# Value and gate projections of sixteen heads: from inside the head loop to a phase of seven half-size products

## The chip, the cores and the metric

The kernel runs on one core of one Trainium2 chip. The metric is the device time of one execution in microseconds (us); lower is better. The engines of the core work in parallel and each takes its own instructions strictly in the order in which they stand: TensorE (PE in the profile; its weight loads are PEld), VectorE (DVE), ScalarE (ACT), GpSimd (POOL) and SyncE (SP). SP issues most of the transfers between DRAM and the on-chip memory (SBUF), POOL issues the rest. [...]

## The reference, cut to what matters

A two-layer network on 1024 latent tokens (plus 256 context tokens) of width 1024. Layer 0 mixes neighbourhood attention and mLSTM heads; the change does not touch its code. Layer 1 is a bidirectional gated recurrence with 16 heads of key width 128 and value width 128. Of the reference, this matters:

```
def project(h):
    q, f_fwd, f_bwd, i, z = _split_cols(h @ w_in, C_SIZES)      # five blocks of 2048 columns
    ...
    rec = (silu(q) per head, i per head, (decay(f_fwd), decay(f_bwd)))
    return rec, z

def merge(o, z):
    o = _rms(o per head, h_norm)
    return (o * jax.nn.silu(z)) @ w_out
```

For head `h`, `q`, `f_fwd`, `f_bwd`, `i` (the value, `v` in the kernel) and `z` (the gate) are each 128 columns of a product of the normalised tokens (1280 x 1024, float32) with a weight matrix (1024 x 10240). `z` is needed for the 1024 latent tokens only, `v` for the context too. Within a head the recurrence over a chunk is computed as a masked product of queries and keys in seven levels (block sizes 1, 2, 4 ... 64), and between chunks as a scan.

## The kernel before, in words

The program is written with a tile framework. A scheduler with a timeline model of the engines orders each engine's instructions before the launch: of the instructions that it holds ready, the one that comes first in the program goes first. Once ordered, each engine runs its list in that order, so an instruction that waits holds up everything behind it on its engine.

Float32 accuracy on PE comes from splits: every operand is kept as a high and a low part in the format fp32r, and a product is three matmuls (high x high, high x low, low x high): lines 120 to 122 in `dense`. `split` (lines 69 to 72) makes the parts of a weight slab of 128 x 512 elements: a copy on ACT (line 71) and a subtraction on DVE (line 72). `wblock` and `wring` load slabs and split them; a ring of `slabs` = 4 buffers for each part holds the weights of two projections of 128 columns.

Layer 0 ends with its output projection (lines 731 to 733, `out_tile`), the normalisation of layer 1 and the transposes that fill `hh` and `hl`, the high and low parts of the normalised tokens, transposed (`mod_tr`, `h_sink`; code lines 1148 to 1156). While PE is at that, the first projections of head 0 are already mixed in (`wf`).

Then the head loop (lines 1163 to 1170) runs 16 times:

- `hg_proj(h)` forms the two decays `F` and the queries `q`: for each direction 256 + 512 + 512 columns of tokens, for the queries 512 + 512, each of 24 matmuls (8 depth steps x 3). Weights stand still in the array, tokens move through.
- `hg_intra` runs the seven levels for two halves of 512 tokens. `hg_level` is a chain across engines: ACT gathers keys (`gksel`, line 895), PE forms scores in four matmuls (line 900), DVE copies the scores of this level under a mask into `A` (line 910) and scales `Q` and `K` in place by four products with the running decay (line 918), which the next level needs.
- `hg_vz(h)` makes `v` and `z`: a block of 256 columns (128 of `v`, 128 of `z`) as four slabs `wzh`, `wzl`; 24 matmuls with 256 moving columns for the context's `v`; then for each of the eight token tiles 24 matmuls of 256 columns (tokens standing still, weights moving), a copy of `v`, a sigmoid and a product for `z` (lines 816 to 821).
- `hg_ctx` forms the state after the context, `hg_scan` runs the scan over eight chunks, the normalisation, the product with `z`, and writes the head's result to DRAM.

Between heads, buffers allow a projection of the next head to start once the first level has read `F`. After the loop the second output projection (lines 731 to 733 again) ends the kernel; its first half of depth (`out_ahead`) is ready before the last head is through and lies mixed with it.

Of the kernel before, what the change touches and what calls it, by code (L numbers as in the profile page):

```python
# [9 lines left out]
F32 = mybir.dt.float32  # L10
F32R = mybir.dt.float32r
U8 = mybir.dt.uint8
AF = mybir.ActivationFunctionType
# [5 lines left out]
P = 128  # L19
# [24 lines left out]
class Prog:  # L44
# [724 lines left out]
            self.nc.sync.dma_start(out=self.gbc[:, v, :], in_=src.partition_broadcast(P))  # L769


    def hg_proj(self, h, pool, w=None):
# [4 lines left out]
        F = [self.t(p, [P, 2, 512], F32, "gF", 1) for p in (pool, self.fp)]  # L777
        Fc = self.t(self.fp, [P, 2, CTX], F32, "gFc", 1)
        todo = [(d, t0, n) for d in range(2) for t0, n in ((LAT, CTX), (512, 512), (0, 512))]
        if w:  # L780

            todo.sort(key=lambda x: x[1] == 0)
        w = w or [None, None]
        for d, t0, n in todo:
            w[d] = w[d] or self.wring([col(1 + d)], P)
            ps = self.ps("mm", [P, n])
            self.proj_tr(ps, w[d], 0, t0, n)
            dst = Fc[:, d, :] if t0 == LAT else F[t0 // 512][:, d, :]
            nc.scalar.activation(dst, ps, AF.Sigmoid)
            nc.vector.tensor_scalar(out=dst, in0=dst, scalar1=olb, scalar2=lb, op0=ALU.mult, op1=ALU.add)  # L790
# [9 lines left out]
        return dict(F=F, Fc=Fc, q=q)  # L800

    def hg_vz(self, h, st, pool):
        nc, a = self.nc, self.a
        col = lambda i: a["wc"][:, i * 2048 + h * P : i * 2048 + (h + 1) * P]
        w = self.wblock(pool, "wz", [col(3), col(4)], KD, 256)
        v = self.t(pool, [P, NT, P], F32, "gv", 2)
        z = self.t(pool, [P, NT - 2, P], F32, "gz", 1)
        ps = self.ps("mm", [P, CTX])
        self.proj_tr(ps, w, 0, LAT, CTX)
        vT = self.t(pool, [P, CTX], F32, "gEc", 1)  # L810
        nc.scalar.copy(vT, ps)
        pt = self.ps("tr", [P, 2, P])
        for j in range(2):
            nc.tensor.transpose(pt[:, j, :], vT[:, j * P : (j + 1) * P], self.ident)
        nc.scalar.copy(v[:, 8:10, :], pt)
        for tt in range(8):
# [4 lines left out]
            nc.vector.tensor_tensor(out=z[:, tt, :], in0=z[:, tt, :], in1=ps[:, P:256], op=ALU.mult)  # L821
        st["v"], st["z"] = v, z


# [157 lines left out]
    def build(self):  # L982
        tc, nc, a = self.tc, self.nc, self.a
        dma = nc.sync.dma_start
        with ExitStack() as es:
# [7 lines left out]
            self.Gd = self.scratch(dr, "Gd", [2, 4, T])  # L993
            self.mpd = self.scratch(dr, "mpd", [2, 4, NT])
            self.x1 = self.scratch(dr, "x1", [T, D])
            self.md_all = self.scratch(dr, "md", [20, T, 256])
            self.md = {}

# [109 lines left out]
            lk = self.fp = l1.enter_context(tc.tile_pool(name="hgk", bufs=1))  # L1108
            with tc.tile_pool(name="op0", bufs=2) as op, ExitStack() as wl:
                self.gate_bc(0, op, 2, 1)  # L1110
                later = []
# [32 lines left out]
                for ld in rest:  # L1144
                    ld()
                self.slabs = 4
                wf = [self.wring([a["wc"][:, 2048 : 2048 + P]], P), None]
# [9 lines left out]
                wf[1] = self.wring([a["wc"][:, 4096 : 4096 + P]], P)  # L1157

            with l1:
                pool = l1.enter_context(tc.tile_pool(name="hg", bufs=2))  # L1160
                self.rawp = pool
                l1.enter_context(self.pp.phase(s=3, acc=1))
                st = self.hg_proj(0, pool, wf)
# [164 lines left out]
```

## Time and profile before

| what | value |
|---|---|
| three runs | 3575.16, 3577.86, 3580.52 us |
| median of the runs | 3577.86 us |
| profiled execution, from its first to its last instruction (span) | 3582.2 us |
| granted TensorE clock, mean over the span | 0.992 |
| head loop, middle heads | 92.2 us each |

The profiled execution has no separate time of its own beside its span; the span lies 4.3 us above the median of the runs. In the profile, `mm<-wzh,hh` means: an instruction writes a buffer named `mm` from buffers named `wzh` and `hh`; `128x256` is partitions x elements, `x64` the number of instructions, and after the bar stand busy time in us and the mean of one in ns. Matmuls are pipelined: the mean of one is longer than the distance between two starts, so rates are read from start times in the timeline.

### The profile page before, as it was taken

Reading aid. Unit: us, or ns where it says so; the run is one execution under the profiler, and the core shown is the slowest. Engines: PE = TensorE matmul, PEld = TensorE weight load, DVE = VectorE, ACT = ScalarE, POOL = GpSimd, SP = SyncE. Lnnn points to the kernel's source line nnn. Section 1 sums busy time; section 2 is a strip of 40 time slices with the busy share of each in tenths; the row PEclk is TensorE's granted clock in tenths of the full one; section 3 lists DMA queues with packets and bytes.
Section 4 is the critical chain, followed back from the end, with each engine's and each line's share of the span. In section 5 each row is a group of like instructions: output and inputs, shape, how many; then the busy total and the mean of one; then the engine's idle time right before and its main releaser. Section 6 shows DMA issues by size and latency. Waiting matters only on the chain.

```text
span 3582.2 us, 65593 instructions
## 1 busy us (share of the span) xinstructions
PE 3517.0 (98%) x24954; PEld 3223.1 (90%) x24954; DVE 2216.3 (62%) x5976; ACT 1419.4 (40%) x3493; POOL 456.2 (13%) x752
## 2 busy tenths in 40 slices
PE   8999999999999999998899999999999999999998
PEld 5879999999999999997788999999999999999877
DVE  5646676666744765655556666666666666666753
ACT  5545555445533333433354333333333333333431
POOL 2222222222211212201010000000000000000000
PEclk9999999999999999999999999999999999999999
DMA  5532222232234434324742111111111111111263
GB/s 211 173 99 77 83 71 81 72 90 76 80 96 145 127 94 140 116 73 149 221 145 77 36 36 34 36 36 36 36 33 36 30 36 36 33 33 36 77 192 117
DMA packets 323051, 305.25 MB, mean 85 GB/s; under 512 B 29016, under 2 KB 280088, under 8 KB 322608
## 3 DMA queue, kind: packets, MB, share of 16 engines
q1 hardware_dynamic: 290704, 217.44, 20.7%
q0 software_dynamic: 32032, 83.61, 6.9%
q8 instruction: 197, 3.23, 0.4%
q14 instruction: 118, 0.97, 0.1%
HBM read 241.49 MB, written 59.30 MB: 84 GB/s over the span
## 4 chain that ended last, share of the span: by engine, by line
PE 85%; issue 6%; DMA 4%; DVE 2%; POOL 1%; ACT 1%; SPq 0%; POOLq 0%; DVEq 0%; ACTq 0%
PE mm L122 18%; PE mm L120 18%; PE mm L121 18%; PE s L900 6%; PE acc L677 2%; PE tr L657 2%; PE mm L731 2%; PE mm L732 2%; PE mm L733 2%; PE acc L461 2%; PE s L470 2%; DMA mld<-md 1%; PE acc L451 1%; PE s L929 1%; PE acc L953 1%
## 5 line engine op out<-in xcount | busy, mean ns | idle before, releaser
L122 PE MATMUL mm<-wh,hl 128*128 128x256 f32 x2560 | 749.6, 293 | 0.3 <-DVE hl L253 0.3
L120 PE MATMUL mm<-wh,hh 128*128 128x256 f32 x2560 | 747.0, 292 | 0.0
L121 PE MATMUL mm<-wl,hh 128*128 128x256 f32 x2560 | 745.9, 291 | 0.0
L122 PEld LDWEIGHTS mm<-wh,hl 128*128 128x128 f32 x2560 | 489.1, 191 | 11.1 <-issue 4.1
L120 PEld LDWEIGHTS mm<-wh,hh 128*128 128x128 f32 x2560 | 489.3, 191 | 7.7 <-issue 1.5
L121 PEld LDWEIGHTS mm<-wl,hh 128*128 128x128 f32 x2560 | 489.2, 191 | 7.1 <-issue 0.5
L120 PE MATMUL mm<-hh,wh 128*128 128x512 f32 (+1 forms) x1216 | 448.3, 369 | 0.0
L121 PE MATMUL mm<-hl,wh 128*128 128x512 f32 (+1 forms) x1216 | 448.3, 369 | 0.0
L122 PE MATMUL mm<-hh,wl 128*128 128x512 f32 (+1 forms) x1216 | 448.1, 368 | 0.0
L122 PE MATMUL mm<-wzh,hl 128*128 128x256 f32 x1024 | 295.3, 288 | 0.0
L120 PE MATMUL mm<-wzh,hh 128*128 128x256 f32 x1024 | 294.2, 287 | 0.0
L121 PE MATMUL mm<-wzl,hh 128*128 128x256 f32 x1024 | 293.9, 287 | 0.0
L895 ACT COPY gksel<-gK 128x512 f32<-128x512 f32 x224 | 149.3, 667 | 315.5 <-PE s L900 159.7
L122 PEld LDWEIGHTS mm<-hh,wl 128*128 128x128 f32 x1216 | 229.7, 189 | 31.4
L120 PEld LDWEIGHTS mm<-hh,wh 128*128 128x128 f32 x1216 | 229.7, 189 | 31.1
L121 PEld LDWEIGHTS mm<-hl,wh 128*128 128x128 f32 x1216 | 229.7, 189 | 30.7
L900 PE MATMUL s<-gQ,gksel 128*128 128x128 f32 x1792 | 254.9, 284 | 0.0
L900 PEld LDWEIGHTS s<-gQ,gksel 128*128 128x128 f32 x1792 | 231.4, 191 | 1.3
L71 ACT CAST wh<-wraw 128x512 fp32r<-128x512 f32 x242 | 148.6, 620 | 202.3 <-PE mm L121 122.5
L731 PE MATMUL mm<-woh,yh 128*128 128x512 f32 x524 | 209.4, 400 | 11.9 <-issue 9.7
L72 DVE TENSOR_TENSOR wl<-wraw,wh 128x512 fp32r<-128x512 f32 x242 | 165.3, 689 | 87.3 <-ACT wh L71 84.9
L733 PE MATMUL mm<-woh,yl 128*128 128x512 f32 x524 | 209.4, 400 | 0.0
(316 smaller groups left out, 7463.0 us busy)
## 6 DMA issues: line engine op xcount, KB each, us to landing
wraw<-yd SPq DMA_DIRECT2D x144, 256.0 KB
wraw<-in_wab_dram SPq DMA_DIRECT2D x112, 256.0 KB
md<-ev POOLq DMA_DIRECT2D x100, 256.0 KB, 2.7
wraw<-in_wc_dram SPq DMA_DIRECT2D x96, 256.0 KB
adar<-in_wada_dram POOLq DMA_DIRECT2D x32, 512.0 KB, 4.6
wraw<-in_wc_dram SPq DMA_DIRECT2D x128, 128.0 KB
adar<-in_wada_dram SPq DMA_DIRECT2D x16, 512.0 KB
wraw<-in_wab_dram SPq DMA_DIRECT2D x64, 128.0 KB
```

The source lines that it names most:

```text
L71: nc.scalar.copy(hi, x)
L72: nc.vector.tensor_tensor(out=lo, in0=x, in1=hi.bitcast(F32), op=ALU.subtract)
L120: mm(ps, lhsT=lh(k), rhs=rh(k), start=(k == 0), stop=False)
L121: mm(ps, lhsT=lh(k), rhs=rl(k), start=False, stop=False)
L122: mm(ps, lhsT=ll(k), rhs=rh(k), start=False, stop=(k == nk - 1))
L461: nc.tensor.matmul(num, lhsT=qc[:, j, :], rhs=C[d][:, j, :], start=False, stop=(j == 1))
L470: nc.tensor.matmul(u, lhsT=st["k"][c][:, j * P : (j + 1) * P], rhs=vw, start=True, stop=True)
L657: nc.tensor.transpose(pt[:nk, i, :], pr[:, o : o + nk], self.ident)
L731: mm(ps, lhsT=yh[:, k, :], rhs=w.h(kk), start=(kk == 0), stop=False)
L733: mm(ps, lhsT=yl[:, k, :], rhs=w.h(kk), start=False, stop=(kk == 8 * len(qs) - 1))
L895: nc.scalar.copy(ksel.rearrange("p (b s i) -> p b s i", s=2, i=h), pick(K))
L900: nc.tensor.matmul(pa[:, c, :].rearrange("p (b s i) -> p b s i", s=2, i=h), lhsT=ksel[:, c * P : (c + 1) * P], rhs=qp[:, c * nbc : (c + 1) ...
```

## The change

- A phase ahead of the head loop computes `v` and `z` of all heads for the 1024 latent tokens and writes them to DRAM (`vzd`). It goes through the 2048 + 2048 columns in eight blocks of 256 + 256.
- The first block (`q_plain`) is computed as before, by 2 x 8 x 24 matmuls; its first weights (`early`) are loaded while layer 0's output projection runs, in place of head 0's first decay weights (`wf`).
- Each of the other seven blocks (`q_seven`) is seen as a product of 2 x 2 halves: tokens (0 to 511, 512 to 1023), depth (0 to 511, 512 to 1023) and columns (`v`, `z`). It is formed by seven products of halves in place of eight, of 4 x 12 matmuls each.
- Four of the seven need sums and differences of halves of the tokens; `q_sums` makes them once, on DVE and ACT, split into high and low parts. Sums of halves of the weights are made for each block (`q_form`), and the products are combined on DVE (`q_out` and the lines around it). Results leave through POOL's DMA queue, 128 transfers of 128 x 256.
- In the loop `hg_vz` loads `v` and `z` of the head by two transfers on SP and still computes the context's `v`, with two slabs of its own from the ring (`wring`) in place of the four of `wz`.
- `hg_proj` loses the early start of head 0, and `F`, `Fc` move into the loop's pool with the same number of buffers. `z` gets two buffers in place of one. During the new phase PSUM has four banks `sa` beside two `mm` and two `tr`.

```
-        w = self.wblock(pool, "wz", [col(3), col(4)], KD, 256)
         v = self.t(pool, [P, NT, P], F32, "gv", 2)
-        z = self.t(pool, [P, NT - 2, P], F32, "gz", 1)
+        z = self.t(pool, [P, NT - 2, P], F32, "gz", 2)
+        for t, i in ((v, 0), (z, 1)):
+            nc.sync.dma_start(
+                out=t[:, 0:8, :], in_=self.vzd[i, :, h * P : (h + 1) * P].rearrange("(c p) f -> p c f", p=P)
+            )
+        w = self.wring([a["wc"][:, 3 * 2048 + h * P : 3 * 2048 + (h + 1) * P]], P)
...
-        for tt in range(8):
-            ps = self.ps("mm", [P, 256])
-            self.proj_nat(ps, w, tt, 0, 256)
-            nc.scalar.copy(v[:, tt, :], ps[:, 0:P])
-            nc.scalar.activation(z[:, tt, :], ps[:, P:256], AF.Sigmoid)
-            nc.vector.tensor_tensor(out=z[:, tt, :], in0=z[:, tt, :], in1=ps[:, P:256], op=ALU.mult)
...
+    def q_form(self, raw, n, add=None):
+        w = _W([], [], 2, 256)
+        for i in range(2):
+            if add:
+                self.nc.vector.tensor_tensor(out=raw[n][i], in0=raw[n][i], in1=raw[add][i], op=ALU.add)
+            w.lo.append(self.t(self.wp, [P, 512], F32R, "wl", self.slabs))
+            w.hi.append(self.t(self.wp, [P, 512], F32R, "wh", self.slabs))
+            self.split(w.hi[i], w.lo[i], raw[n][i])
+        return w
...
+        def product(a, w):
+            for i in range(4):
+                ps = self.q_ps()
+                self.q_mul(ps, a(i), w, True, True)
+                yield i, ps
+
+        u, v, m5 = {}, {}, {}
+        for i, ps in product(lambda i: self.q_h(i, 0), self.q_form(raw, "11")):
+            u[i] = self.t(pool, [P, 256], F32, "qu", 4)
+            nc.scalar.copy(u[i], ps)
+        for i, ps in product(lambda i: self.q_h(i, 1), self.q_form(raw, "21")):
+            self.q_out(pool, i, j, 0, u[i], ps, ALU.add)
+        for i, ps in product(s("1"), self.q_form(raw, "11", "12")):
+            m5[i] = ps
+        for i, ps in product(s("2"), self.q_form(raw, "11", "22")):
+            tt(out=u[i], in0=u[i], in1=ps, op=ALU.add)
+            v[i] = self.t(pool, [P, 256], F32, "qv", 4)
+            tt(out=v[i], in0=m5[i], in1=u[i], op=ALU.subtract)
+        for i, ps in product(s("3"), self.q_form(raw, "12", "22")):
+            self.q_out(pool, i + 4, j, 1, v[i], ps, ALU.subtract)
+            tt(out=u[i], in0=u[i], in1=ps, op=ALU.add)
+        for i, ps in product(lambda i: self.q_h(i + 4, 1), self.q_form(raw, "11", "21")):
+            self.q_out(pool, i + 4, j, 0, u[i], ps, ALU.add)
+        for i, ps in product(s("4"), self.q_form(raw, "22")):
+            self.q_out(pool, i, j, 1, v[i], ps, ALU.add)
...
+                with tc.tile_pool(name="qv", bufs=1) as pool, self.pp.phase(sa=4):
+                    self.q_plain(0, early, pool)
+                    S = self.q_sums(pool)
+                    for j in range(1, 8):
+                        self.q_seven(j, S, pool)
```

More of the change, by code (lines that the diff above doesn't have):

```diff
@@ L776, in hg_proj @@
         lb, olb = self.lb[:, 0, h : h + 1], self.lb[:, 1, h : h + 1]
-        F = [self.t(p, [P, 2, 512], F32, "gF", 1) for p in (pool, self.fp)]
-        Fc = self.t(self.fp, [P, 2, CTX], F32, "gFc", 1)
+        F = [self.t(pool, [P, 2, 512], F32, "gF", 2) for _ in range(2)]
+        Fc = self.t(pool, [P, 2, CTX], F32, "gFc", 1)
         todo = [(d, t0, n) for d in range(2) for t0, n in ((LAT, CTX), (512, 512), (0, 512))]
-        if w:
-            todo.sort(key=lambda x: x[1] == 0)
-        w = w or [None, None]
+        w = [None, None]
         for d, t0, n in todo:
@@ new lines, in q_raw @@
+    def q_raw(self, pool, j):
+        nc, raw = self.nc, {}
+        for n in ("11", "21", "12", "22"):
+            c0 = (3 if n[1] == "1" else 4) * 2048 + j * 256
+            raw[n] = []
+            for i in range(2):
+                r = self.t(pool, [P, 512], F32, f"b{n}", 4 if n == "11" else 2)
+                k0 = (int(n[0]) - 1) * 512 + i * 256
+                nc.sync.dma_start(
+                    out=r.rearrange("p (k f) -> p k f", f=256),
+                    in_=self.a["wc"][k0 : k0 + 256, c0 : c0 + 256].rearrange("(k p) f -> p k f", p=P),
+                )
+                raw[n].append(r)
+        return raw
@@ new lines, in q_form, with q_mul @@
+    def q_form(self, raw, n, add=None):
+        w = _W([], [], 2, 256)
+        for i in range(2):
+            if add:
[4 more added lines that the diff above has]
+        return w
+    def q_mul(self, ps, a, w, first, last):
+        mm = self.nc.tensor.matmul
+        ah, al = a
+        for k in range(4):
+            mm(ps, lhsT=ah[:, k, :], rhs=w.h(k), start=first and k == 0, stop=False)
+            mm(ps, lhsT=ah[:, k, :], rhs=w.l(k), start=False, stop=False)
+            mm(ps, lhsT=al[:, k, :], rhs=w.h(k), start=False, stop=last and k == 3)
@@ new lines, in q_ps, with q_plain @@
+    def q_ps(self):
+        self.nq += 1
+        return self.ps("sa" if self.nq % 8 < 4 else "mm" if self.nq % 2 else "tr", [P, 256])
+    def q_plain(self, j, early, pool):
+        raw = self.q_raw(pool, j)
+        for z in range(2):
+            w = early if early and not z else [self.q_form(raw, f"{k}{z + 1}") for k in (1, 2)]
+            for c in (4, 0):
+                for i in range(4):
+                    ps = self.ps("sa", [P, 256])
+                    for k in range(2):
+                        self.q_mul(ps, self.q_h(c + i, k), w[k], k == 0, k == 1)
+                    self.q_out(pool, c + i, j, z, ps)
@@ new lines, in q_seven @@
+    def q_seven(self, j, S, pool):
+        nc = self.nc
+        raw = self.q_raw(pool, j)
+        s = lambda n: lambda i: [t[:, :, i * P : (i + 1) * P] for t in S[n]]
+        tt = nc.vector.tensor_tensor
+        def product(a, w):
+            for i in range(4):
+                ps = self.q_ps()
[20 more added lines that the diff above has]
+            self.q_out(pool, i, j, 1, v[i], ps, ALU.add)
@@ L1146, in build @@
                 self.slabs = 4
-                wf = [self.wring([a["wc"][:, 2048 : 2048 + P]], P), None]
+                early = []
+                for k in range(2):
+                    rows = a["wc"][k * 512 : (k + 1) * 512, 3 * 2048 : 3 * 2048 + 256]
+                    early.append(self.wblock(self.wp, "w", [rows], 4, 256, op, ring=self.slabs))
                 for tt in [8, 9, 4, 5, 6, 7, 0, 1, 2, 3]:
```

57 lines of the change are left out of this document (52 added, 5 removed).

## The prediction

> **What bounds the kernel now.** I read the page first (busy shares, chain), then stages of the span, then one middle head by shapes, then that head's timelines of TensorE and VectorE.
>
> ```profile
> span 3582.2 us, 65593 instructions
> PE 3517.0 (98%) x24954; PEld 3223.1 (90%) x24954; DVE 2216.3 (62%) x5976; ACT 1419.4 (40%) x3493; POOL 456.2 (13%) x752
> ...
> PE 85%; issue 6%; DMA 4%; DVE 2%; POOL 1%; ACT 1%; SPq 0%; POOLq 0%; DVEq 0%; ACTq 0%
> ...
> L122 PE MATMUL mm<-wzh,hl 128*128 128x256 f32 x1024 | 295.3, 288 | 0.0
> L120 PE MATMUL mm<-wzh,hh 128*128 128x256 f32 x1024 | 294.2, 287 | 0.0
> L121 PE MATMUL mm<-wzl,hh 128*128 128x256 f32 x1024 | 293.9, 287 | 0.0
> L71 ACT CAST wh<-wraw 128x512 fp32r<-128x512 f32 x242 | 148.6, 620 | 202.3 <-PE mm L121 122.5
> L72 DVE TENSOR_TENSOR wl<-wraw,wh 128x512 fp32r<-128x512 f32 x242 | 165.3, 689 | 87.3 <-ACT wh L71 84.9
> ...
> md<-ev POOLq DMA_DIRECT2D x100, 256.0 KB, 2.7
> ```
>
> PE holds 85% of the chain. The three rows of 1024 are the work that the change moves: 3072 matmuls, 192 a head. The stages (columns: span; busy of PE, PEld, DVE, ACT, POOL; clock; DMA share; GB/s):
>
> ```profile
> 1778.00:1791.00 13.00, 3.26 (x9) 2.40 (x8) 6.05 (x9) 3.66 (x7) 0.54 (x1) 0.60 0.74 242
> 1852.00:1948.00 96.00, 96.00 (x472) 80.88 (x471) 60.22 (x150) 50.55 (x124) 8.46 (x18) 1.00 0.39 117
> 2500.07:2592.27 92.20, 92.20 (x652) 86.07 (x652) 60.40 (x150) 29.99 (x74) 4.28 (x6) 1.00 0.12 35
> 3376.00:3389.00 13.00, 12.47 (x58) 10.25 (x59) 10.00 (x21) 7.32 (x12) 0.00 (x0) 0.87 1.03 311
> ```
>
> A middle head is 92.2 us with PE full; DVE is busy 60.4. An average hides that DVE's work is not spread evenly over the head. Shapes of that head, and PE's and DVE's timelines in its seven levels:
>
> ```profile
> L120 PE MATMUL mm<-wzh,hh 128*128 128x256 f32 x64 | 18.4, 287 | 0.0
> L900 PE MATMUL s<-gQ,gksel 128*128 128x128 f32 x114 | 16.4, 285 | 0.0
> L895 ACT COPY gksel<-gK 128x512 f32<-128x512 f32 x14 | 9.3, 667 | 20.9 <-PE s L900 10.3 <-issue 5.0 <-DVE gK L861 3.2
> L918 DVE TENSOR_TENSOR gK<-gK,gT 128x256 f32<-128x256 f32 x24 | 9.0, 417 | 0.0
> L910 DVE COPY_PREDICATED gA<-glm,s 128x512 f32<-128x512 uint8 x12 | 8.9, 742 | 4.3 <-PE s L900 4.1
> L973 DVE SCALAR_TENSOR_TENSOR gyn<-acc,gss,gz 128x128 f32<-128x128 f32 x8 | 2.4, 345 | 0.9 <-POOL gss L147 0.6 <-PE tr L976 0.3
> L959 DVE SCALAR_TENSOR_TENSOR gS<-gS,gT,s 128x128 f32<-128x128 f32 x7 | 2.4, 347 | 7.6 <-PE acc L954 5.2 <-PE s L957 2.4
> L147 POOL TENSOR_TENSOR gss<-gss,mhalf 128x4 f32<-128x4 f32 x2 | 2.4, 1194 | 0.2
> L979 POOL DMA_DIRECT2D yd<-gyt x2 | 1.2, 600 | 19.4 <-ACT gyt L978 10.6 <-DVE gz L821 8.8
> L835 DVE TENSOR_SCALAR gq<-gFc 128x512 f32<-128x512 f32 x1 | 0.4, 414 | 0.0
> L790 DVE TENSOR_SCALAR gF<-gF,lb 128x512 f32<-128x512 f32 x4 | 2.2, 542 | 0.0
> ```
>
> ```profile
> 2508.25 0.61 PE L929 MATMUL s<-gq,gksel 128*128 128x128 f32 x4
> ...
> 2515.12 0.28 PE L121 MATMUL mm<-wzl,hh 128*128 128x256 f32 x1
> ...
> 2517.96 0.28 PE L121 MATMUL mm<-wzl,hh 128*128 128x256 f32 x1
> 2518.08 1.06 PE L900 MATMUL s<-gQ,gksel 128*128 128x128 f32 x8
> 2518.89 0.36 PE L122 MATMUL mm<-wzh,hl 128*128 128x256 f32 x1
> ...
> 2539.23 1.06 PE L900 MATMUL s<-gQ,gksel 128*128 128x128 f32 x8
> ```
>
> ```profile
> 2519.17 0.75 DVE L910 COPY_PREDICATED gA<-glm,s 128x512 f32<-128x512 uint8 x1 [0.94 <-PE s L900]
> 2519.82 0.73 DVE L918 TENSOR_TENSOR gQ<-gQ,gT 128x256 f32<-128x256 f32 x2
> 2520.48 0.74 DVE L918 TENSOR_TENSOR gK<-gK,gT 128x256 f32<-128x256 f32 x2
> 2521.15 0.27 DVE L821 TENSOR_TENSOR gz<-gz,mm 128x128 f32<-128x128 f32 x1
> 2521.35 0.73 DVE L910 COPY_PREDICATED gA<-glm,s 128x512 f32<-128x512 uint8 x1
> ```
>
> From 2515.12 to 2517.96 stand 25 matmuls of 256 columns: 0.118 us from start to start (their mean of 287 ns is pipelined). A score group costs PE 0.81 us (2518.08 to 2518.89). A masked copy and two pairs of products per half level cost DVE 0.65 + 0.66 + 0.67 = 1.98 us. So in the levels DVE is nearly always busy, and PE's own share, 0.81 in about 2 us, is less than half. The rest of PE's time there is filled by exactly the matmuls that the change takes out: between 2508.25 (behind the first level's groups) and 2539.23 (the last group) lie 149 matmuls of `hg_vz`.
>
> **The change, part by part.**
>
> *PE's count.* Out: 3072 x 0.118 = 362.5 us. In: the plain block 2 x 8 x 24 = 384, seven blocks of 7 x 4 x 12 = 336, together 2736, x 0.118 = 322.8. The shape is the same (128 x 128 standing, 256 moving). Net **-39.7 us**.
>
> *The head loop without its filler.* In the order in which the changed kernel's instructions stand on PE, the score groups of levels 1 to 6 of heads 1 to 14 follow each other with nothing between them but the 24 matmuls of the context's `v`, two pairs of transposes, and near the end the transposes of `K`; the next head's projections stand in front of this stretch or behind it. Working per head:
> - PE's own work without the 192: 92.2 - 22.7 = 69.5 us.
> - Of it inside the stretch: 30.98 us (2508.25 to 2539.23) - 149 x 0.118 = 13.4, plus 24 x 0.118 = 2.8 for the context: 16.2. Outside: 53.3, still back to back as far as the order shows.
> - DVE's list inside it, between the scores of level 0 and the last group: 24 pairs (L918) x 0.66 = 15.9, 13 masked copies x 0.64 = 8.3, four `gyn` (0.345 each), one level-0 product, one `gF` (0.542), one `gq` (0.414): about 2.8. Sum **27.0 us**, on one engine in order. PE cannot leave it sooner, since the last group needs the last but one pair.
> - Handing over at both ends 0.6 us (a group's 1.06 us against its 0.81, and a wait on ACT).
>
> Period 53.3 + 27.0 + 0.6 = 80.9. DVE's waits for PE inside the stretch were 4.1 us a head (L910's row); without the filler in PE's queue they should shrink, but a group still needs a 0.667 us gather on ACT first. Bounds 0 to 4.1; I take 1.3, nearer to none because what DVE waited for was mostly the filler: **82.2 us, PE idle 12.7** (11.4 to 15.5). Times 14 heads: **+178** (160 to 217). What DVE sheds per head, two slab splits and eight gate products, lies mostly outside the stretch and is worth nothing while PE is the bound there.
>
> *Head 0 and head 15.* Head 0's levels have projections of head 1 between them, and head 15's the second output projection's first half (192 matmuls), which before covered head 15's scan. That scan then stands bare: seven state steps of PE and DVE (L959, 0.347 us, plus a matmul and handing over, about 0.8 each), two normalisations with POOL's 1.2 us, the write (2.7 us to land) and reading back. About 25 us, of which PE's own matmuls fill some 10. **+15** (5 to 25).
>
> *The new phase.* Per seven-product block PE 336 x 0.118 = 39.6 us. DVE: 14 low parts and 8 sums of 128x512 x 0.689 + 36 combinations of 128x256 x 0.42 = 30.3. ACT: 14 x 0.62 and twelve copies or sigmoids of 256 columns, each under the 0.667 of L895's 512: at most 16.7. POOL: 16 issues x 0.6 = 9.6, with nothing else on its queue. SP: eight loads of 256 KB. The ring holds two products' weights, so a product's split (2 x (0.62 + 0.69) = 2.6 us) runs under the product before it (5.7 us). All of it is under PE; I cost it at nothing, and if that cover failed it would be up to 2.6 us per product (below). Three places are not covered:
> - the raw weights of the plain block's second half: they wait until the projection's buffers are free, 2 MB at the 240 GB/s of the stage around 1780 take 8 us, against 11 us of PE work at hand, partly waiting itself: +6 (0 to 12);
> - `q_sums`: 56 operations of DVE of 128x512, with the splits and combinations around them about 45 us, while PE has about 49 us that doesn't need them: +5 (0 to 15);
> - the seam into the loop: head 0's first weights go into memory that the phase's results occupy, so they wait for the last result's way (two DVE operations 0.84, sigmoid at most 0.67, issue 0.6, landing 2.7), then load 2.7 and split 1.3: +10 (3 to 15).
>
> Together **+21** (3 to 42). Head 0's early projections leave the stretch 1852 to 1948, where PE is full; the plain block's first matmuls take their place, both are PE work: 0. The two loads of `v`, `z` per head (1 MB) run two heads ahead on a DMA system used to 12%: 0; a late one would hold the scan.
>
> *Sum.* 3582.2 - 39.7 + 178 + 15 + 21 = 3756.5 against this execution's span; the median of the runs lies 4.3 lower: **3752 us**, 4.9% slower. With the lower bounds 3706, with the upper ones 3837.
>
> **The clock.** PE idle for a moment has a price here:
>
> ```profile
> 3376.53 1.16 PE L847 MATMUL s<-gv,gknc 128*128 128x128 f32 x8 [1.88 <-ACT gknc L842]
> ```
>
> After these 1.88 us the stage 3376 to 3389 ran at 0.87, that is 3.4 of 13 us at half. In the bare levels PE's gaps are shorter, about 1 us, but come every 2 us. [...] No stage of this trace has such a rhythm. I leave it out of the sum and make it a rival.
>
> **Rivals.**
> 1. *The clock drops in the bare levels.* Then PE's 16.2 us there grow up to 32 and pass DVE's 27: +5 us, and 3.4 us at half behind them: +1.7. Up to 6.7 x 14 = 94: 3846 us. For it: the 1.88 us gap. [...] Chance 0.13.
> 2. *The new phase starves PE.* DVE's list (30 of 39.6 us) mixes splits with combinations that wait for PE; if half of each split lies open: 49 products x 1.3 = 64, 3816 us. For it: ACT and DVE rows 71 and 72 wait for each other even now. Chance 0.10.
> 3. *Faster: PE stays full in the levels after all*, because DVE's gathered waits vanish and the next head's decays run under the levels. Period 69.5, phase and tail at their lower bounds: 3582.2 - 39.7 + 8 - 4.3 = 3546 us. It decides only if the idle per head falls under (39.7 - 21 - 15) / 14 = 0.3 us, so a period under 70. Against it: DVE's 27.0 us for 16.2 of PE, by count. Chance 0.03.
>
> **Numbers.** The forecast has 0.73; 0.01 is left for no change. What a measurement of this kernel can tell from none is about 0.2%, 7 us. The forecast's own range is 3706 to 3837; 3700 to 3840 takes in the second rival and part of the first. Faster 0.03, same 0.01, slower 0.96.
>
> **What would show it.** Right: middle heads of 81 to 84 us, in each a stretch of about 27 us with PE half idle behind DVE and score groups some 2 us apart; the new phase full on PE with products of 5.7 us; matmuls 336 fewer. Wrong: a period near 70 (rival 3), a clock under 0.95 in the loop (rival 1), PE idle between products with ACT or DVE as releaser (rival 2), or idle PE outside the levels, where I assume none.

## The result, and the profile after

The changed kernel takes **3824.19 us** (median of four executions, 3822.89 to 3830.06) where the kernel before takes 3579.19 (four executions, 3575.16 to 3580.75): **6.9% slower**, ratio 1.0688 with a 95% interval of 1.0672 to 1.0703. The forecast was 3752, with a range of 3700 to 3840. The side came out as foretold, and so did the mechanism in the head loop. But 72 us are missing from the sum, and most of them lie where the prediction had written a zero.

From the page of the changed kernel: span, busy time and instructions of each engine, the chain of waits that ended last, by engine ("issue" is time for which the profile shows no wait), and four groups (busy us and mean ns, then idle time before them and what ended it).

```profile
span 3820.8 us, 65738 instructions
PE 3586.6 (94%) x24618; PEld 3229.4 (85%) x24618; DVE 2385.5 (62%) x6294; ACT 1456.6 (38%) x3427; POOL 517.8 (14%) x880
...
PE 26%; issue 11%; DVE 11%; DMA 5%; POOL 2%; ACT 1%; SPq 0%; POOLq 0%; DVEq 0%; ACTq 0%
...
L120 PE MATMUL mm<-hh,wh 128*128 128x512 f32 (+1 forms) x1344 | 487.8, 363 | 34.4 <-ACT gFc L786 26.5
...
L1027 PE MATMUL s<-gQ,gksel 128*128 128x128 f32 x1792 | 293.3, 316 | 79.6 <-DVE gQ L1045 52.7
...
L731 PE MATMUL mm<-woh,yh 128*128 128x512 f32 x524 | 214.5, 410 | 52.2 <-ACT yh L71 35.7
...
L71 ACT CAST yh<-wraw 128x512 fp32r<-128x512 f32 x144 | 86.7, 619 | 214.3 <-DMA wraw<-yd 117.7
```

PE has the 336 matmuls fewer that were counted (24954 to 24618), and is busy for 94% of the span instead of 98%. The 26% of the chain must not be set beside the 85% of before: on this page the chain is followed back only to 1680 us, 56% of the span. From 1680 us to the end, PE holds 87% of the chain before and 46% after. So PE no longer bounds that part alone. Two of the waits are large; the same groups in the kernel before:

```profile
L900 PE MATMUL s<-gQ,gksel 128*128 128x128 f32 x1792 | 254.9, 284 | 0.0
...
L731 PE MATMUL mm<-woh,yh 128*128 128x512 f32 x524 | 209.4, 400 | 11.9 <-issue 9.7
```

Score groups (L1027; L900 before) now stand 79.6 us idle, mostly behind DVE: the levels of the head loop. And the matmuls of layer 0's output projection (L731) stand 52.2 us idle, 35.7 of them behind the splits of its `y` tiles, which in turn wait for loads: work that the change does not touch.

The stages of both kernels, cut at the same instructions: the first matmul of the last pass of layer 0's output projection, the last transposes of that stage (L229), the context transposes of head 0 and of head 14 (columns: span; busy PE, PEld, DVE, ACT, POOL; clock; DMA share; GB/s). Before:

```profile
0.00:1788.00 1788.00, 1738.25 (x13226) 1598.96 (x13227) 1088.44 (x3253) 810.54 (x2043) 365.81 (x612) 0.99 0.38 113
1788.00:1918.40 130.40, 130.39 (x615) 108.75 (x616) 76.16 (x182) 68.34 (x173) 13.71 (x28) 0.98 0.44 131
1918.40:1997.40 79.00, 79.00 (x544) 73.58 (x543) 56.81 (x139) 29.54 (x67) 0.00 (x0) 1.00 0.17 48
1997.40:3286.30 1288.90, 1288.90 (x9092) 1203.27 (x9091) 844.25 (x2100) 419.19 (x1021) 60.42 (x84) 1.00 0.12 35
3286.30:3582.20 295.90, 280.50 (x1482) 238.55 (x1480) 150.66 (x304) 91.83 (x190) 16.27 (x28) 0.98 0.40 121
```

After:

```profile
0.00:1789.50 1789.50, 1734.37 (x13226) 1594.65 (x13226) 1087.61 (x3253) 809.24 (x2043) 365.40 (x612) 0.99 0.37 114
1789.50:1978.30 188.80, 152.62 (x655) 107.18 (x656) 78.96 (x180) 69.40 (x170) 12.23 (x28) 0.98 0.29 88
1978.30:2398.10 419.80, 402.97 (x3124) 391.46 (x3123) 290.04 (x612) 139.39 (x277) 68.98 (x128) 0.98 0.29 97
2398.10:3557.00 1158.90, 1051.12 (x6414) 932.51 (x6413) 784.65 (x1960) 353.54 (x770) 54.27 (x84) 0.96 0.15 45
3557.00:3820.80 263.80, 245.55 (x1205) 203.60 (x1203) 144.27 (x290) 85.01 (x168) 16.91 (x28) 0.98 0.42 133
```

The differences of these rows against the terms of the prediction. A head's place against its context moved a little with the change, so the two outer stages are taken together; the forecast for them is 322.8 (the phase) + 21 + 15 - 2 x 22.65 (the products that left heads 0 and 15).

| stage | forecast | measured |
|---|---|---|
| up to the last pass of layer 0's projection | 0 | +1.5 |
| that pass | 0 | **+58.4** |
| new phase, lead-in of head 0, and all behind head 14 (+340.8 and -32.1) | +313.5 | +308.7 |
| 14 periods of the head loop | -139.1 | -130.0 |
| sum (span) | +174.4 | +238.6 |

So three questions went to the chip: what the 58.4 us are, whether the rest has the causes that the prediction gave, and whether the heads can have their filler back.

### The profile page after: what moved, and what is told of

The parts are those of the page before. It is cut to its first block, busy times and chain, and to the rows that moved or that the text cites. A ratio compares the mean times of both kernels' runs of the same rounds, so it can differ in the third digit from the quotient of the medians.

```text
span 3820.8 us, 65738 instructions
## 1 busy us (share of the span) xinstructions
PE 3586.6 (94%) x24618; PEld 3229.4 (85%) x24618; DVE 2385.5 (62%) x6294; ACT 1456.6 (38%) x3427; POOL 517.8 (14%) x880
## 4 chain that ended last, share of the span: by engine, by line
PE 26%; issue 11%; DVE 11%; DMA 5%; POOL 2%; ACT 1%; SPq 0%; POOLq 0%; DVEq 0%; ACTq 0%
PE mm L120 6%; PE mm L121 6%; PE mm L122 6%; DMA wraw<-yd 3%; DVE gQ L1045 3%; DVE gK L1045 3%; DVE gA L1037 2%; PE s L1027 2%; POOL vzd L883 2%; PE mm L731 1%; PE mm L733 1%; PE mm L732 1%; PE acc L1080 1%; PE acc L1081 1%; PE s L1067 1%
## 5 line engine op out<-in xcount | busy, mean ns | idle before, releaser
L120 PE MATMUL mm<-hh,wh 128*128 128x512 f32 (+1 forms) x1344 | 487.8, 363 | 34.4 <-ACT gFc L786 26.5
L122 PE MATMUL mm<-hh,wl 128*128 128x512 f32 (+1 forms) x1344 | 487.5, 363 | 0.0
L121 PE MATMUL mm<-hl,wh 128*128 128x512 f32 (+1 forms) x1344 | 487.0, 362 | 0.0
L1027 PE MATMUL s<-gQ,gksel 128*128 128x128 f32 x1792 | 293.3, 316 | 79.6 <-DVE gQ L1045 52.7
L1027 PEld LDWEIGHTS s<-gQ,gksel 128*128 128x128 f32 x1792 | 260.9, 215 | 109.0 <-ACT gksel L1022 69.3
L120 PEld LDWEIGHTS mm<-hh,wh 128*128 128x128 f32 x1344 | 257.1, 191 | 71.4 <-ACT gFc L786 29.4
L121 PEld LDWEIGHTS mm<-hl,wh 128*128 128x128 f32 x1344 | 257.3, 191 | 34.4
L731 PE MATMUL mm<-woh,yh 128*128 128x512 f32 x524 | 214.5, 410 | 52.2 <-ACT yh L71 35.7
L732 PE MATMUL mm<-wol,yh 128*128 128x512 f32 x524 | 209.0, 399 | 0.0
L731 PEld LDWEIGHTS mm<-woh,yh 128*128 128x128 f32 x524 | 99.9, 191 | 88.0 <-ACT yh L71 53.4
L71 ACT CAST yh<-wraw 128x512 fp32r<-128x512 f32 x144 | 86.7, 619 | 214.3 <-DMA wraw<-yd 117.7
```

The source lines that it names most:

```text
L71: nc.scalar.copy(hi, x)
L120: mm(ps, lhsT=lh(k), rhs=rh(k), start=(k == 0), stop=False)
L121: mm(ps, lhsT=lh(k), rhs=rl(k), start=False, stop=False)
L122: mm(ps, lhsT=ll(k), rhs=rh(k), start=False, stop=(k == nk - 1))
L731: mm(ps, lhsT=yh[:, k, :], rhs=w.h(kk), start=(kk == 0), stop=False)
L732: mm(ps, lhsT=yh[:, k, :], rhs=w.l(kk), start=False, stop=False)
```

## Experiments

**Where the 58.4 us come from.** In the changed kernel the pass's chain of waits no longer runs through PE (start, length in us, what):

```profile
1853.10 0.63 ACT yh L71
...
1854.47 2.82 DMA wraw<-yd
...
1857.31 0.63 ACT yh L71
...
1857.96 0.70 DVE yl L72
1858.68 2.81 DMA wraw<-yd
...
1861.57 0.63 ACT yh L71
```

Load, copy, subtraction, next load: one after the other, 4.2 us a round, as if there were one buffer for the raw `y` tiles. The pool has three (`wraw`). Its readers and writers in this pass, same kernel (xcount: least/median/most ns, first and last start):

```profile
L71 ACT CAST yh<-wraw x40: 617/618/621, 1788.8 to 1966.8; 128x512 fp32r<-128x512 f32 x40
...
L718 SPq DMA_DIRECT2D wraw<-yd x39: 359/360/1449, 1790.2 to 1964.0; - x39
L71 ACT CAST wh<-wraw x2: 621/622/622, 1970.1 to 1970.8; 128x512 fp32r<-128x512 f32 x2
```

The two splits of weights at 1970.1 and 1970.8 stand behind the last `y` tile. My theory was this. The ring for split weights has four slabs a part, and this pass still uses two of them for its own last slabs; `early` loads two blocks of two slabs. The first block finds slabs, the second only when the pass is over, and until then its two raw slabs lie in two of the three raw buffers. In the kernel before, `wf` took only the two slabs that were free.

*Raw buffers of their own for the early weights:*

```
-                    early.append(self.wblock(self.wp, "w", [rows], 4, 256, op, ring=self.slabs))
+                    early.append(self.wblock(self.wp, "w", [rows], 4, 256, op, 2, "eraw", ring=self.slabs))
```

> The changed kernel, with raw buffers of its own (two) for the first two weight blocks of the new phase, which are loaded during the layer-0 output projection. Theory A (these two blocks sit in two of the three raw buffers until that projection's slabs are free, so the y tiles are loaded and split one after the other through the third): the projection's last stage goes from 188.8 back to about 131 to 135 us, and the time from 3824 to about 3765 to 3770. Rival B (the stage is longer because other work stands in it: more loads and splits of weights on ScalarE and VectorE, or the projections of the plain block queued there): the stage stays above 175 us and the time at 3810 to 3825.

Measured: 3749.44 us (3746.22 to 3753.11), 75 less than the changed kernel; against the kernel before 1.0474 (1.0458 to 1.0489).

*Only the first early block ahead of the tiles, the second behind them:*

```
-                for k in range(2):
+                for k in range(1):
...
                     self.mod_tr(1, [xn], tt, op, self.h_sink(tt * P, P))
+                rows = a["wc"][512:1024, 3 * 2048 : 3 * 2048 + 256]
+                early.append(self.wblock(self.wp, "w", [rows], 4, 256, op, ring=self.slabs))
```

> The changed kernel, with only the first of the two early weight blocks loaded ahead of the tiles of the layer-0 output projection, the second behind them. Theory A (raw buffers held): the first block takes the slabs that are free and gives its raw buffers back at once, so the stage is again 131 to 135 us long; what is loaded later costs at most 3 us at the start of the phase: about 3765 to 3772. Rival B (other work in the stage): half of the 58 us comes back at most, 3795 to 3824.

Measured: 3772.21 us (3769.26 to 3774.48), 52 less; 1.0537 (1.0519 to 1.0554). It is 23 above the first cure: 8 in front of the first tile, 8 in head periods of 83.1 in place of 82.5, the rest behind head 14.

*The kernel before, with one raw buffer for `y`:*

```
-            yr = self.t(rp or yp, [P, 512], F32, "wraw", 3).rearrange("p (j t) -> p j t", j=4)
+            yr = self.t(rp or yp, [P, 512], F32, *(("yraw", 1) if getattr(self, "oneraw", 0) else ("wraw", 3))).rearrange("p (j t) -> p j t", j=4)
...
+                self.oneraw = 1
                 for tt in [8, 9, 4, 5, 6, 7, 0, 1, 2, 3]:
```

> The kernel before, in which the y tiles of the layer-0 output projection go through one raw buffer of their own instead of sharing three. Nothing else is changed. Theory A: one raw buffer alone makes the stage as long as in the changed kernel, about 185 to 190 us instead of 130.4, and the time 3634 to 3640 instead of 3579. Rival B: the loads stay hidden behind the matmuls of each tile, the stage stays at 130 to 140 us and the time below 3590.

Measured: 3621.48 us (3612.92 to 3624.57), 1.0112 (1.0097 to 1.0127): slower by 42, not by 55 to 60.

The transposes of the pass's ten tiles tell the pace (first and last start), in this order: before, the changed kernel, own raw buffers, one early block, the kernel before with one buffer. One fence for each:

```profile
L229 PE MATMUL tr<-ident,nx x80: 270/272/276, 1811.3 to 1918.4; 128*128 128x128 f32 x80
```

```profile
L229 PE MATMUL tr<-ident,nx x80: 270/272/273, 1815.2 to 1978.3; 128*128 128x128 f32 x80
```

```profile
L229 PE MATMUL tr<-ident,nx x80: 270/272/276, 1799.1 to 1906.1; 128*128 128x128 f32 x80
```

```profile
L229 PE MATMUL tr<-ident,nx x80: 270/272/276, 1806.7 to 1914.0; 128*128 128x128 f32 x80
```

```profile
L229 PE MATMUL tr<-ident,nx x80: 270/272/276, 1800.6 to 1964.8; 128*128 128x128 f32 x80
```

Ten tiles take 107.1, 163.1, 107.0, 107.3 and 164.2 us. Both cures give the pace back whole, and one raw buffer in the kernel before, without anything of the change, makes the whole loss: **the cause is the number of raw buffers that the `y` tiles find free**, and rival B of the three expectations is out. The single-buffer kernel shows the same wait, a 2.8 us load between two splits of each `y` tile:

```profile
L71 ACT CAST yh<-yraw 128x512 fp32r<-128x512 f32 x36 | 22.2, 618 | 69.5 <-DMA yraw<-yd 64.0 <-PE mm L733 3.4 <-PE mm L732 2.0
```

My sizes missed by what stands ahead of the pass. With raw buffers of its own (third and fifth row) the first tile is 11 to 12 us earlier than before; so the first cure gave 75 us and not 55 to 60, and the single buffer cost 42 and not 55. The prediction had shown that hole without asking for its cause: the row 1778 to 1791, PE busy 3.26 of 13 us.

*The kernel before, with two raw buffers for `y` and two for the weights in place of three shared:*

```
-            rw = rawp if isinstance(rawp, list) else (rawp or self.rawp, rawb, rawt)
+            rw = rawp if isinstance(rawp, list) else (rawp or self.rawp, getattr(self, "rb", rawb), rawt)
...
-            yr = self.t(rp or yp, [P, 512], F32, "wraw", 3).rearrange("p (j t) -> p j t", j=4)
+            yr = self.t(rp or yp, [P, 512], F32, *(("yraw", 2) if getattr(self, "oneraw", 0) else ("wraw", 3))).rearrange("p (j t) -> p j t", j=4)
...
-                raws[:] = [op, 3, "wraw"]
+                raws[:] = [op, 2, "wraw"]
+                self.rb = 2
...
+                self.oneraw = 1
```

> The kernel before, in which the y tiles of the layer-0 output projection have two raw buffers of their own and the weights two others, instead of three shared. Nothing else changes. In the runs with y buffers of their own the first tile's transposes stood at 1799 to 1801 us instead of 1811, also where y had only one. Theory A (the start of that stage waits for raw buffers that weights hold): with two y buffers the tiles keep 12 us each and the start is 11 to 12 us earlier, 3566 to 3570 instead of 3579.6. Rival B (the 12 us at the start are taken back in front of the head loop, as 6.5 of the 46.4 us were in the run with one buffer, or two buffers are too few for a tile in 12 us): 3575 to 3590.

Measured: **3567.40 us** (3564.53 to 3568.86), 0.9958 (0.9944 to 0.9972): the one version here that is faster than both kernels. It differs from the kernel before in two things at once: the pools are separate, and there are four raw buffers in place of three. Which of the two gives the 14 us was not tried apart. The same 13 us in it, PE full where it had been idle:

```profile
1778.00:1791.00 13.00, 13.00 (x59) 10.72 (x58) 5.18 (x8) 3.98 (x7) 0.54 (x1) 1.00 0.79 234
```

**What the seven products are worth.** All eight blocks computed plainly:

```
-                    S = self.q_sums(pool)
                     for j in range(1, 8):
-                        self.q_seven(j, S, pool)
+                        self.q_plain(j, None, pool)
```

> The changed kernel, in which all eight column blocks of the new phase are computed plainly (no sums of halves, no seven products). 336 matmuls more of 0.118 us are +39.6 us; without the sums of x ahead of the phase about -5. Theory A (the phase is bound by TensorE): 3824 + 35 = 3855 to 3864. Rival B (the seven products pay their saving back to VectorE and ScalarE, which make the sums and put the products together): 3815 to 3835, no more than 10 us above the changed kernel.

Measured: 3872.38 us (3871.86 to 3872.60), 48 above the changed kernel (1.0816, 1.0800 to 1.0833). The phase with the lead-in of head 0:

```profile
1981.30:2441.20 459.90, 444.32 (x3460) 433.71 (x3458) 126.36 (x262) 115.03 (x247) 69.25 (x128) 0.98 0.26 88
```

459.9 against 419.8: +40.1 for 336 matmuls, 0.119 us each. PE bounds the phase, and the saving arrives whole, although with the seven products DVE has 290.0 us of work in place of 126.4. So rival B is out; but the 5 us that I had set for `q_sums` are not there either. The other 8 us, by which it is above theory A's figure too, are mostly the 14 head periods, which came out at 83.1 instead of 82.8 (+5).

**What bounds a head.** In the changed kernel a middle head takes 82 to 84 us. PE's waits in one of them (head from 2565.6):

```profile
L120 PE MATMUL mm<-hh,wh 128*128 128x512 f32 x48 | 19.7, 411 | 1.8 <-ACT gFc L786 1.8
...
L1027 PE MATMUL s<-gQ,gksel 128*128 128x128 f32 x112 | 17.9, 309 | 6.0 <-DVE gQ L1045 3.6 <-ACT gksel L1022 1.6 <-DVE gQ L991 0.6
```

The kernel with raw buffers of its own for the early weights has nearly the same heads (82.5 us in the mean of 14, against 82.8) and is the base of what follows. The core of its levels, and the rest of the head behind them:

```profile
2712.90:2729.10 16.20, 13.84 (x85) 12.53 (x86) 16.20 (x42) 5.69 (x10) 0.00 (x0) 0.79 0.05 18
2729.10:2737.35 8.25, 5.89 (x29) 4.60 (x28) 4.45 (x12) 1.19 (x4) 0.00 (x0) 1.00 0.01 2
```

DVE is busy 16.20 of 16.20 us, as the prediction had it. What its sum had not (it stood there as rival 1): the clock of 0.79, that is 6.8 us at half. To see whether DVE's list sets the time, its products of one level were left out, from this base and from the kernel before (the output is then another one):

```
             (Qv, 0, 0, Tv[:, 1, :, 1]), (Qv, 1, 1, Tv[:, 0, :, 0]),
         ):
+            if lev == 3:
+                continue
```

> The changed kernel with raw buffers of its own for the early weights, in which the fourth of the seven levels leaves out its multiplications of K and Q by the segment products (the output is then another one). That takes eight VectorE instructions of about 0.41 us from each head, 3.3 us, and nothing from TensorE or ScalarE. Theory A (in the levels VectorE's list sets the period now that the value and gate products are gone): the middle heads go from 82.5 to about 79 us and the time from 3749 to about 3698 to 3704. Rival B (what binds a level is the round from its matmuls over ScalarE's copy to the next matmuls, or TensorE's own work): periods 81.5 to 82.5 us, 3735 to 3750.

> The kernel before with the same eight multiplications left out of each head (the output is then another one). Theory A (TensorE is full in its levels, and VectorE's list lies beside it): periods stay at 92.0 to 92.3 us and the time within 5 us of 3580. If VectorE's list counted here too, 3.3 us a head would show: 3530.

Measured: in the base 3732.41 us (3729.22 to 3735.08), 17 less and not 45 to 51, between the two theories and nearer to B; periods of 81.6 to 82.3. In the kernel before 3578.58 (3576.11 to 3582.80), ratio 1.0004 (0.9994 to 1.0013): nothing, as both had it. The same two windows of a head without the products:

```profile
2707.70:2723.90 16.20, 13.19 (x92) 12.12 (x92) 15.47 (x38) 6.31 (x11) 0.00 (x0) 0.89 0.05 18
2723.90:2732.00 8.10, 6.34 (x21) 4.99 (x22) 2.63 (x8) 0.68 (x3) 0.00 (x0) 0.79 0.01 2
```

From the diagonal's scores behind the first level (L1056) to the last score group it is 24.3 to 25.1 us, against 26.4: in the mean of 14 heads the levels are 1.8 us shorter, for 2.5 us less of DVE in the head shown (53.47 against 55.98). In the kernel before, where PE is full, the same cut changes nothing. So DVE does set the levels. But the clock moved: 3.4 us at half are now in the window *behind* the levels (0.79 of 8.1), in every head. What that costs can be read from the base itself. Four of its 14 heads have such a spell behind the levels and take 83.4 to 83.8 us, the other ten 81.8 to 82.3: 1.3 to 1.7 us. So the head keeps 0.6 us of its 1.8 (81.9 in the mean against 82.5). My expectation priced DVE and left the clock out.

Then idle matmuls in the levels, to keep PE busy and to see whether the clock then stays up, with and without the cut:

```
         pa = self.ps("s", [P, 4, P])
+        if lev:
+            for c in range(4):
+                nc.tensor.matmul(pa[:, c, :], lhsT=self.ident, rhs=self.ident, start=True, stop=True)
```

> The run with the eight multiplications left out, and ahead of the four matmuls of each half's level (levels 2 to 7) four idle matmuls of the identity with itself into the same PSUM tile, which the true ones then write over: 48 matmuls a head, 0.11 us each, 5.3 us of TensorE work that stands where TensorE waits for VectorE. Theory C (VectorE does set the levels, which were 2.0 us shorter without the multiplications, but a half-clock window of 3.4 us behind the levels took 1.7 us of it back; with TensorE kept busy the clock stays at full speed): no half-clock windows in most heads, periods 79.5 to 80.5 us instead of 81.9, the time 3700 to 3715 instead of 3732. Rival B (a level is bound by its own round, or by TensorE's work): the added matmuls lengthen the heads, periods 82 to 87 us, 3735 to 3800.

> The changed kernel with raw buffers of its own for the early weights and the same idle matmuls, nothing left out. Theory C: the half-clock windows of 6.8 us in the levels go, but they lay beside VectorE's list and cost nothing; only the four heads of 83.4 to 83.8 us, which had a second window behind the levels, fall to 82: periods 81.5 to 82.1 us, the time 3738 to 3749 instead of 3749. Rival B: the added 5.3 us of TensorE work show, periods 84 to 88 us, 3775 to 3830. If the clock had cost its whole window (6.8 us at half speed, 3.4 us a head), periods would fall to 78.6 and the time to 3700.

Measured: 3786.88 us (3783.38 to 3791.54) and 3799.81 (3794.98 to 3801.30), both slower; the middle heads take 83.5 to 85.1 us, and 85.3. A head of the second, in the levels and behind them:

```profile
2713.50:2723.50 10.00, 10.00 (x89) 10.00 (x88) 9.76 (x26) 3.70 (x6) 0.85 (x1) 1.00 0.20 59
2723.50:2739.70 16.20, 16.20 (x147) 16.20 (x146) 15.31 (x40) 6.09 (x10) 0.61 (x1) 1.00 0.11 38
...
2744.70:2748.20 3.50, 3.02 (x7) 2.44 (x8) 1.35 (x4) 0.66 (x2) 0.00 (x0) 0.51 0.00 0
```

The half clock is gone from the levels (1.00 twice), but the added matmuls were more than the gap. I had counted 48 a head, 5.3 us; in the trace there are 96, since each of these float32 matmuls stands there twice, and at 0.11 us each that is 10.6 us. PE is now full in the levels, its busy time rises by 7.5 us a head (82.43 against 74.88), the levels grow to 28.3 us, and a half-clock spell lands behind them. My theory C misses by 50 to 90 us, and the times are in rival B's ranges, though for the reason that TensorE was overfilled. So these runs don't tell what the half clock in the levels costs by itself. The base gives a hint: of the four heads with 3.4 us at half behind the levels, two have 6.8 us at half in the levels and take 83.8 us, two have 3.4 there and take 83.4. By these four heads, 3.4 us at half cost 0.4 us in the levels; no run changed the clock alone.

**Can the heads have their filler back?** The base kernel with two buffers for `Fc`, so that the next head's projections need not wait for this head's context:

```
-        Fc = self.t(pool, [P, 2, CTX], F32, "gFc", 1)
+        Fc = self.t(pool, [P, 2, CTX], F32, "gFc", 2)
```

> The kernel with raw buffers of its own for the early weights, and two buffers instead of one for the forget-gate columns (gFc) of a head, so that the next head's projections need not wait for this head's context. Theory A (the middle heads of the changed kernel are 82.5 us because TensorE has nothing to do in the levels once the value and gate projections are gone, and the next head's projections could be that filler, but for Fc): part of TensorE's 8 us of gaps in a head closes, periods 74 to 80 us, the time 3749 less 14 x (2.5 to 8.5), 3630 to 3714. Rival B (the period is bound by VectorE or by the round of a level's matmul, ScalarE, VectorE and back, so filler changes nothing): periods 81 to 83 us, 3725 to 3752.

Measured: 3791.28 us (3789.24 to 3792.26): 42 *slower* than its base, periods 85.3 to 85.4, which neither theory had. PE's waits in a head, and four windows from the next head's start to just behind its end:

```profile
L1027 PE MATMUL s<-gQ,gksel 128*128 128x128 f32 x112 | 16.1, 288 | 2.7 <-DVE gQ L991 1.2 <-DVE gT L1047 0.8 <-ACT gkn L1008 0.7
...
L1079 PE MATMUL acc<-gv,gA 128*128 128x128 f32 x16 | 3.2, 282 | 2.6 <-DVE gA L1037 2.6
...
L967 PE MATMUL tr<-ident,gq 128*128 128x128 f32 x5 | 1.5, 431 | 5.7 <-DVE gq L963 5.7
```

```profile
2678.50:2707.40 28.90, 25.78 (x147) 23.03 (x148) 11.35 (x30) 4.50 (x14) 1.22 (x2) 0.91 0.07 19
2707.40:2710.80 3.40, 3.40 (x18) 3.40 (x17) 1.11 (x3) 0.00 (x0) 0.00 (x0) 0.50 0.00 0
2710.80:2762.00 51.20, 46.12 (x297) 41.17 (x295) 41.60 (x103) 21.21 (x41) 2.43 (x4) 1.00 0.21 62
2762.00:2768.80 6.80, 4.96 (x24) 4.99 (x25) 2.38 (x7) 0.96 (x2) 0.00 (x0) 0.50 0.01 2
```

The scores' wait does fall (2.7 us, against 6.0 in the changed kernel's head above and 4.8 in one of the base). But the projections had covered DVE's work behind the levels; now that stands bare (2.6 and 5.7 us), and in nearly every head the clock is at half for 3.4 us with PE full and for 6.8 us behind the levels.

The context's column factor in a buffer of its own as well:

```
-        k = self.t(pool, [P, 2, CTX], F32, "gq", 2)
+        k = self.t(pool, [P, 2, CTX], F32, "gkc", 1)
```

> As the run before, and the column factor of the context in a buffer of its own instead of the one that it shares with the levels, so that the next head's projections stand in more of the levels. Theory A: periods 70 to 77 us, the time 3749 less 14 x (5.5 to 12.5), 3574 to 3672. Rival B: periods 81 to 83 us, 3725 to 3752.

Measured: 3752.16 us (3750.12 to 3755.36), no gain over the base; periods mostly 82.0 to 83.6, with half-clock spells in two places of each head.

And the next head's projections straight behind the level products:

```
                 for h in range(16):
                     hv = self.hg_intra(st, pool)
+                    nst = self.hg_proj(h + 1, pool) if h < 15 else None
                     self.hg_vz(h, st, pool)
...
-                    if h < 15:
-                        st = self.hg_proj(h + 1, pool)
+                    st = nst
```

> As the run before, with the next head's projections issued straight behind the level products in the program, so that they fill all the levels, and nothing is left to fill the scan behind them. Theory A: the levels cost TensorE nothing but its own work, periods 70 to 75 us where the scan does not wait, 3574 to 3644; if the scan, bare now, waits for VectorE in its place, some 5 us a head come back, 3644 to 3714. Rival B: 81 to 83 us, 3725 to 3752.

Measured: 3705.29 us (3704.09 to 3707.10), 44 less than the base, 1.0345 (1.0330 to 1.0361) against before. Nearly all periods are 78.7 to 80.2, above theory A's first figure. The time is in the range of its second branch, a bare scan, but not for that cause, as a head from 2589.1 shows:

```profile
L120 PE MATMUL mm<-hh,wh 128*128 128x512 f32 x48 | 19.5, 405 | 1.6 <-ACT gFc L786 1.6
...
L1027 PE MATMUL s<-gQ,gksel 128*128 128x128 f32 x112 | 15.9, 286 | 1.2 <-DVE gQ L991 1.2
L120 PE MATMUL mm<-hh,wh 128*128 128x256 f32 x24 | 7.8, 324 | 1.6 <-ACT gF L786 1.6
```

No score group waits for the levels' products (L1045) any more, here as in the two runs before it, so the missing filler was the cause of that wait. Only here does it show in the period: a head of the run before still had 1.7 us of waiting for the last masked copy behind the levels (L1079) and a second half-clock spell. But PE is still busy only 73.7 of 78.7 us in the next head. Its waits are now mostly for the decays (L786, 3.2 us) and for the start of the levels (L991, 1.2), and only 0.7 us are in the scan's lines. This is the best version of the change tried here, and it stays behind the kernel before.

## Why the prediction was right, and where it was wrong

- **The failing step** stands behind the sum of the new phase: "Head 0's early projections leave the stretch 1852 to 1948, where PE is full; the plain block's first matmuls take their place, both are PE work: 0." It weighed the matmuls that changed places and not the loads that came with them. `early` needs four slabs where `wf` took two, and so holds two raw buffers of a pool that the `y` tiles share: +58.4 us. The prediction had listed in the sum every place where the *new* work might wait; it had not asked which old work waits for the buffers that the new loads take. With this term put right the sum is 3756.5 + 58.4 = 3815 against the span of 3820.8; the rest is 9 us more in the heads, 5 less in the phase and the tail, and 1.5 ahead of the pass.
- **That the time fell into the stated range is luck.** The range was wide for the heads, the phase and the tail, and these came out within 10 us of their forecasts; the 58.4 us come from a term that had no bounds at all. The upper bound is mis-added besides: 3582.2 - 39.7 + 217 + 25 + 42 - 4.3 is 3822, not 3837. The measured 3824.19 lies just above that sum, and below 3840 only by the slip and the room given to rivals.
- **PE's count: right.** 336 matmuls fewer, and the seven products save 40.1 us against 39.6.
- **The head loop without its filler: right in mechanism, 9 us off in size.** A period of 82.2 was forecast; the 14 measured 82.8 in the mean. The stretch came out shorter (26.4 us against 27.0 + 0.6 + 1.3): DVE is busy in all but 0.3 us of it, and its list is a little shorter than counted. The rest of the head came out longer: not "back to back", but with 1.8 us behind `Fc`, which has one buffer and waits for the context's scan, and with half-clock spells there in five of the 14 heads, which take 83.4 to 83.7 (the first 85.5) instead of 82.1.
- **The new phase: +21 was about right in size, in part for another cause.** From 1978.3 to 2308.3 us 2640 of its matmuls stand (the other 96 in the pass before); at 0.118 us they are 311.5 of these 330.0, so +18. The seam into the loop was 7.8 us (forecast 10), its chain as described: result, landing, load, split. The 6 us for late raw weights did not show. In their place PE waited 4.6 us for a free `sa` buffer: the copies of the plain block's first results stand on ACT behind the last tile of the pass. That the two figures are close is luck. `q_sums` cost 0.8 us (forecast 5). Once started, the phase is full:

```profile
1983.20:2032.00 48.80, 48.79 (x394) 48.80 (x395) 42.32 (x72) 22.11 (x44) 10.54 (x20) 0.97 0.42 147
2032.00:2300.50 268.50, 267.77 (x2248) 267.16 (x2246) 187.70 (x401) 86.46 (x173) 57.35 (x107) 1.00 0.28 98
2300.50:2308.30 7.80, 0.00 (x0) 0.00 (x0) 0.86 (x4) 1.03 (x2) 1.08 (x2) 0.76 0.42 134
```

- **Head 15 and the tail** cannot be cut from head 0's lead-in; together with the phase they came to 308.7 against 313.5.
- **Rival 1, the clock: right that it drops, wrong on most of the price.** Every one of the 14 heads has at least 6.8 us at half clock. In nine they lie in the levels alone, and these heads take 82.1 us, next to the 82.2 of the sum without any half clock: the rival's +5 us for the levels did not come, since the stretch stayed at DVE's 26.4 us. The other five have 3.4 us behind the levels, which the rival had priced at 1.7, and this part is about right: together they lift the mean by 0.7 us, to 82.8.
- **Rival 2, the phase starves PE: did not happen** (267.77 of 268.50 us busy). **Rival 3, PE stays full: did not happen.** Its point of decision was a period under 70 us; even with the next head's projections put under the levels on purpose it was 78.9.

## What to carry to other kernels

When loads are added or moved ahead, follow each to the buffer it lands in and ask when that buffer comes free: a load whose consumer must wait holds its landing buffer hostage, and everything that shares the pool slows down, however little the engines changed. Loads of different urgency get buffers of their own; here that, with one raw buffer more in all, made the kernel before 0.4% faster. And before matmuls are taken out of a loop that looks bound by TensorE, find out which of another engine's work they covered: of 22.65 us of matmuls taken out of each head, only 9.3 came off its time.

## What the runs showed of the hardware

In each of the 14 head periods of the changed kernel TensorE's clock was at half for 6.8 us or more, though no idle time of PE in them is longer than 1.94 us. In the traces of the two kernels the 38 spells at half that end inside the trace last 3.41 us (18 of them), 6.83 (15), 10.24 (2) or 13.65 (3).

What went with a spell differed with its place. In the base kernel of the experiments the four heads with 3.4 us at half behind the levels took 83.4 to 83.8 us, the other ten 81.8 to 82.3: 1.3 to 1.7 us more. Among those four, 3.4 us more at half in the levels, where DVE was busy 16.20 of 16.20 us in the head shown, went with 0.4 us more (83.8 against 83.4).
